# Weights in half-size pieces, and four instead of five seven-product pairs in the gate groups of a decoder layer

## The chip, the cores and the metric

The program runs on one core of a Trainium2 chip. Its engines are TensorE (PE: matmuls; PEld: its weight loads), VectorE (DVE), ScalarE (ACT), GpSimd (POOL) and SyncE (SP), which issues most of the loads. The metric is device time in microseconds (us), the median of several executions. Before the change it is 2157.74 us (three runs, 2157.62 to 2161.36).

## What is computed

One layer of a decoder on 272 positions (16 meta tokens and 256 of the sequence), model width 2048, all in float32:

```python
u = rms_norm(h, ffn1_norm_g[l])
h = h + 0.5 * swiglu(u, ffn1_w_gate[l], ffn1_w_up[l], ffn1_w_down[l])      # width 5632
u = rms_norm(h, mix_norm_g[l])
z = u @ w_in[l]
q, k, v, qi, ki, wi, xc, gate_b, gate_c, ga, gc = jnp.split(z, SPLIT_POINTS, axis=-1)
y_attn = dsa_sparse_attention(q, k, v, qi, ki, wi, k_sel) @ w_attn_branch[l]   # top 64 keys
y_conv = (gate_b * causal_depthwise_conv(gate_c * xc, conv_w[l], conv_b[l])) @ w_conv_branch[l]
merged = jax.nn.sigmoid(ga) * y_attn + jax.nn.sigmoid(gc) * y_conv
h = h + merged @ w_out[l]
u = rms_norm(h, ffn2_norm_g[l])
h = h + 0.5 * swiglu(u, ffn2_w_gate[l], ffn2_w_up[l], ffn2_w_down[l])
```

The part around the change is the gates, ga and gc, of 2048 columns each, with their branch products (y_attn and y_conv).

## The kernel before

**Precision.** Every float32 product is made of three matmuls. A weight is split into a rounded part (whi, by ACT) and the rest (wlo, by DVE); the activations are split in the same way; the three are hi x hi, hi x lo and lo x hi.

**The stream of weights.** The class `Stream` holds one list of loads (`loads`) and one of pieces to split (`subs`), in the order of use. A load brought 2048 columns (1 MB) or 1536 (768 KB) into one of RAW_BUFS = 3 buffers of 2048 columns; a piece ("unit") is at most 1024 columns, in one of four split buffers. `next()` gives the next block of weights. When it begins a unit it runs, in this order: what was put up with `early`; one due step; `split` for the unit three further on (whi on ACT, wlo on DVE); then what was put up with `later` and has come due. So the order on ACT and DVE follows from the lags of these calls, and each engine goes through its list in order. `load` issues on SP; a load waits until its buffer's last split is done.

**The stages.** FFN 1 (all 272 positions); the attention projections with the index and attention work between the units; the convolution; the gates, in four groups of 512 columns; the output projection (`po`); FFN 2. From `widen` on, in FFN 2, one more raw buffer and two more split buffers are in use.

**Pairs.** A gate group computes ga and gc for 512 columns and 256 tokens, and goes through the 2048 rows in eight pairs. A plain pair ("C") is eight products of 128x512 blocks, 24 matmuls, in two units, from one 1 MB load. A pair with seven products ("P") saves a product with sums of weights and sums of tokens: 21 matmuls, in four units, from two loads: four sums of weights (1 MB) and three plain blocks (768 KB). The sums of weights are made much earlier (`prepare`): POOL fetches a chunk, DVE does four additions of 512 columns, POOL stores it in a scratch in DRAM. Most preparations are spread over FFN 1, the last LATE of them over the projections. The sums of tokens (`sums_of_tokens`, put into the tiles made) are made by ACT and DVE in the first gate group, at given lags.

**Banks.** The eight PSUM banks of a group are q1 to q8. The seven products go to q1, q3, q5, q6, q7, q4, q2, in the order q7, q5, q6, q3, then the rest; a plain pair uses q2 and q3, then q4 and q8. After the last P pair, `recombine` copies q1 (ACT) and makes four steps on DVE, one per unit: vv from q6, vx from q7, vv from q5, ve from q5. After the eighth pair come the branch products (`pbr`), in four of the banks, 96 matmuls per group from four 1 MB loads; then `merge` on DVE: four multiplies that read these banks, two additions. The merged result of one group is transposed on TensorE inside the next (`turn_merged`, tiles pt, two blocks of four transposes in two banks); ACT and DVE then split it into ms.

Of the kernel before, what the change touches and what calls it, by code (L numbers as in the profile page):

```python
# [15 lines left out]
P = 128  # L16
# [30 lines left out]
RAW_BUFS = 3  # L47
# [13 lines left out]
SEVEN = (3, 5, 7, 1, 6)  # L61
SEVEN2 = (3, 5, 7, 1)
DOUBLES = 2
LATE = 9
# [7 lines left out]
def pairs_gate(c):  # L72
    return list(zip("CCCPPPCC", [0, 2, 4, 3, 5, 7, 6, 1]) if c == 0 else zip("PPCPPPCC", [3, 5, 0, 7, 1, 6, 2, 4]))
# [24 lines left out]
class Stream:  # L98
# [20 lines left out]
    def add(self, src, n, width):  # L119

        per = min(SUB // width, SUB // P)
        g = len(self.loads)
        self.loads.append((src, n * width))
        for k in range(0, n, per):
            self.subs.append((g, "raw", k * width, min(per, n - k), width))

    def add_pair(self, kind, four, five, ahead=None):

        if kind == "C":
            self.add(four.pop(0), 4, WIDE)  # L130
            return
        if kind == "P":
            src, made = ahead.pop(0)
            self.ahead_of.append(src)
            self.made_ahead.append(made)
            self.add(made, 4, WIDE)
            self.add(src[:, WIDE:], 3, WIDE)
            return
        g = len(self.loads)
        src = five.pop(0)  # L140
        self.loads.append((src[:, 2 * WIDE :], 3 * WIDE))
        self.added[g] = len(self.doubles)
        self.doubles.append((g, src))
        self.subs += [
            (g, "sa", 0, 2, WIDE), (g, "sb", 0, 2, WIDE),
            (g, "one", 0, 2, WIDE), (g, "last", 2 * WIDE, 1, WIDE),
        ]

    def widen(self, raw_pool, split_pool, sum_pool):

        self.raw_pools, self.raw_bufs = [raw_pool] + self.raw_pools * 3, RAW_BUFS + 1
        self.split_pools, self.ahead = [split_pool] + self.split_pools * 2, AHEAD + 2
        self.n_raw = self.n_tiles = 0
        self.sum_pool = sum_pool
        self.add_up(DOUBLES - 1)
# [38 lines left out]
    def load(self, upto):  # L194
        while self.n_loaded < min(upto, len(self.loads)):
            src, n = self.loads[self.n_loaded]
            pool = self.raw_pools[self.n_raw % len(self.raw_pools)]
            self.n_raw += 1
            raw = pool.tile([P, RAW], F32, name="raw")
            self.nc.sync.dma_start(raw[:, :n], src)  # L200
            self.raw[self.n_loaded] = raw
            self.n_loaded += 1

    def sum_ahead(self):

        add = self.nc.vector.tensor_add
        for g, kind, _, _, _ in self.subs[self.n_split : self.n_split + 2]:
            if kind == "sa" and self.sum_pool and g not in self.summed:
                self.load(g + self.raw_bufs)
                self.summed.add(g)  # L210
                raw = self.raw[g]
                sb = self.sum_pool.tile([P, 2 * WIDE], F32, name="sb", tag="sb")
                add(sb[:, :WIDE], self.sums[g, "sa"][:, WIDE:], raw[:, :WIDE])
                add(sb[:, WIDE:], sb[:, :WIDE], raw[:, 2 * WIDE : 3 * WIDE])
                self.sums[g, "sb"] = sb

    def split(self, upto):
        nc = self.nc
        while self.n_split < min(upto, len(self.subs)):
# [3 lines left out]
            g, kind, c, kk, width = self.subs[self.n_split]  # L223
            self.load(g + self.raw_bufs)
            n = kk * width
            if (g, kind) in self.sums:
                raw = self.sums.pop((g, kind))
            else:
                raw = self.raw[g][:, c : c + n]
# [63 lines left out]
def tile_decoder_layer(  # L293
# [442 lines left out]
    with ExitStack() as mix:  # L736
# [438 lines left out]
        for at, (i, to) in zip((0, 3, 7, 14, 20), made1.items()):  # L1175
            sums_of_tokens(i, gains[1], to, at)
# [15 lines left out]
        def gates(c):  # L1192
# [3 lines left out]
            def after_end(q, buf, tags):  # L1196
# [12 lines left out]
                lambda n: n == 6 and c > 0 and turn_merged(("q1", "q6")), None, after_end,  # L1209
            )  # L1210

            sides = [[[bank(tag, "pbr"), 0, KC] for tag in tags] for tags in (("q1", "q5"), ("q6", "q7"))]
# [55 lines left out]
    raw2 = ctx.enter_context(tc.tile_pool(name="raw2", bufs=1, reuse_waits="tile"))  # L1268
# [285 lines left out]
```

## Time and profile before

| | |
|---|---|
| runs | 2157.74 us, median of 3 (2157.62 to 2161.36) |
| the profiled execution | 2167.35 us; its span 2165.6 us |
| TensorE busy | 2129.0 us, 98% of the span, 12994 matmuls |
| DVE / ACT busy | 74% / 51% |
| mean granted TensorE clock | 0.995 |
| moved by DMA | 583 MB, 269 GB/s over the span |
| busy share of DVE in FFN 2 (1470 to 2150) | 568 of 680 us |

A page of the profile names engine, source line (L236 is line 236), operation and tiles as out<-in. Idle time of an engine counts only where it is the one that the end waits for. A wait is shown as "engine line <- what ended it: us in total, times, longest". In a timeline the row gives the start, the duration, and in brackets the idle time before it with what ended it.

### The profile page before, as it was taken

The page shows a single profiled execution, that of the slowest core. Times are in us where ns is not written, and L with a number is a line of the kernel's source. Part 1 is how long each engine was busy: PE and PEld are TensorE (multiplying, and loading weights), DVE is VectorE, ACT ScalarE, POOL GpSimd, SP SyncE. Part 2 cuts the span into 40 slices and gives each one's busy share as a digit, 9 for nine tenths or more (in the row PEclk, how much of TensorE's full clock was granted, in tenths as well). Part 3 has the DMA queues.
Part 4 walks back from the last instruction along what each step waited for, and adds up shares of the span by engine and source line. Part 5 has one row for each costly group of instructions (what it writes and reads, how often), then busy time and mean ns, then how long its engine had stood idle before and what let it go on. Part 6 is the DMA issues. An engine that isn't in the chain of part 4 may idle for free.

```text
span 2165.6 us, 32506 instructions
## 1 busy us (share of the span) xinstructions
PE 2129.0 (98%) x12994; PEld 1913.1 (88%) x12994; DVE 1611.4 (74%) x2108; ACT 1112.2 (51%) x1441; POOL 117.0 (5%) x182
## 2 busy tenths in 40 slices
PE   8999999999999999999999998999999999999999
PEld 8999999999999998789987776888888888888887
DVE  7777766677777757787576666587888978888887
ACT  5444433344444445465465454476666566656564
POOL 3000000000000100000000000000000000000000
PEclk9999999999999999999999999999999999999999
DMA  7788888888888867854566576467788887688774
GB/s 279 282 326 335 339 329 332 324 335 332 338 335 322 315 226 284 333 182 138 173 226 220 204 255 233 141 235 266 263 291 256 266 300 288 260 235 304 277 252 146
DMA packets 87702, 583.33 MB, mean 269 GB/s; under 512 B 9760, under 2 KB 9888, under 8 KB 27520
## 3 DMA queue, kind: packets, MB, share of 16 engines
q1 hardware_dynamic: 67680, 446.46, 57.2%
q0 software_dynamic: 19728, 134.64, 17.6%
q8 instruction: 101, 1.65, 0.3%
q14 instruction: 49, 0.40, 0.1%
q10 hardware_dynamic: 144, 0.17, 0.0%
HBM read 516.23 MB, written 65.01 MB: 268 GB/s over the span
## 4 chain that ended last, share of the span: by engine, by line
PE 89%; DVE 4%; DMA 4%; ACT 2%; issue 1%; POOL 0%; SPq 0%; ACTq 0%; DVEq 0%; POOLq 0%
PE q L627 12%; PE q L629 12%; PE q L628 12%; PE pd L418 4%; PE pd L416 4%; PE pd L417 4%; PE pu L417 4%; PE pu L418 4%; PE pu L416 4%; PE pg L417 4%; PE pg L418 4%; PE pg L416 4%; PE po L431 3%; DVE wlo L236 2%; PE po L433 1%
## 5 line engine op out<-in xcount | busy, mean ns | idle before, releaser
L236 DVE TENSOR_TENSOR wlo<-raw,whi 128x1024 fp32r<-128x1024 f32 (+1 forms) x873 | 1007.6, 1168 | 502.9 <-ACT whi L235 493.0
L235 ACT ACTIVATE whi<-raw 128x1024 fp32r<-128x1024 f32 (+1 forms) x873 | 875.0, 1013 | 927.4 <-PE q L629 248.0
L628 PE MATMUL q<-wlo,act 128*128 128x512 f32 x748 | 293.1, 392 | 2.4 <-DVE wlo L236 2.3
L627 PE MATMUL q<-whi,act 128*128 128x512 f32 x748 | 294.2, 393 | 0.8 <-ACT whi L235 0.8
L629 PE MATMUL q<-whi,act 128*128 128x512 f32 x748 | 292.7, 391 | 0.0
L416 PE MATMUL pd<-mid,whi 128*128 128x272 f32 x704 | 201.7, 286 | 0.0
L417 PE MATMUL pd<-mid,whi 128*128 128x272 f32 x704 | 201.7, 286 | 0.0
L418 PE MATMUL pd<-mid,wlo 128*128 128x272 f32 x704 | 201.7, 286 | 0.0
L416 PE MATMUL pg<-act,whi 128*128 128x272 f32 x672 | 192.7, 287 | 0.0
L417 PE MATMUL pg<-act,whi 128*128 128x272 f32 x672 | 192.5, 287 | 0.0
L418 PE MATMUL pg<-act,wlo 128*128 128x272 f32 x672 | 192.5, 287 | 0.0
L416 PE MATMUL pu<-act,whi 128*128 128x272 f32 x672 | 192.5, 286 | 0.0
L417 PE MATMUL pu<-act,whi 128*128 128x272 f32 x672 | 192.5, 286 | 0.0
L418 PE MATMUL pu<-act,wlo 128*128 128x272 f32 x672 | 192.5, 286 | 0.0
L628 PEld LDWEIGHTS q<-wlo,act 128*128 128x128 f32 x748 | 141.5, 189 | 32.6 <-DVE wlo L236 3.8
L627 PEld LDWEIGHTS q<-whi,act 128*128 128x128 f32 x748 | 141.6, 189 | 30.9 <-ACT whi L235 1.9
L180 DVE TENSOR_TENSOR prep<-prep 128x512 f32<-128x512 f32 x240 | 164.2, 684 | 5.5 <-DMA prep<-in_w2p_dram 5.5
L629 PEld LDWEIGHTS q<-whi,act 128*128 128x128 f32 x748 | 141.3, 189 | 29.7
L416 PEld LDWEIGHTS pd<-mid,whi 128*128 128x128 f32 x704 | 132.6, 188 | 0.0
L417 PEld LDWEIGHTS pd<-mid,whi 128*128 128x128 f32 x704 | 132.6, 188 | 0.0
L418 PEld LDWEIGHTS pd<-mid,wlo 128*128 128x128 f32 x704 | 132.6, 188 | 0.0
L416 PEld LDWEIGHTS pg<-act,whi 128*128 128x128 f32 x672 | 126.6, 188 | 0.0
(281 smaller groups left out, 3819.9 us busy)
## 6 DMA issues: line engine op xcount, KB each, us to landing
raw<-in_wgu_dram SPq DMA_DIRECT2D x87, 1024.0 KB, 6.7
raw<-in_w_dram SPq DMA_DIRECT2D x74, 1024.0 KB, 7.0
raw<-in_wd_dram SPq DMA_DIRECT2D x44, 1024.0 KB, 6.5
prep<-in_w2p_dram POOLq DMA_DIRECT2D x42, 1024.0 KB, 9.5
s<-prep POOLq DMA_DIRECT2D x42, 1024.0 KB, 6.7
raw<-s SPq DMA_DIRECT2D x42, 1024.0 KB, 5.8
raw<-in_w2p_dram SPq DMA_DIRECT2D x42, 768.0 KB, 5.6
raw<-in_wcv_dram SPq DMA_DIRECT2D x24, 1024.0 KB, 4.9
```

Source lines behind the costliest of these rows:

```text
L180: nc.vector.tensor_add(x[out], x[a], x[b])
L235: nc.scalar.activation(to[0], raw, AF.Copy)
L236: nc.vector.tensor_sub(to[1], raw, to[0].bitcast(F32))
L416: nc.tensor.matmul(ps, whi, xhi, start=first, stop=False)
L417: nc.tensor.matmul(ps, whi, xlo, start=False, stop=False)
L418: nc.tensor.matmul(ps, wlo, xhi, start=False, stop=last)
L431: nc.tensor.matmul(ps.rearrange("p (a t) -> p a t", a=2), whi, x(i), start=i == 0, stop=False)
L433: nc.tensor.matmul(ps[:, :SEQ], wlo, x(i)[:, 0, :], start=False, stop=i == total - 1)
L627: nc.tensor.matmul(ps, xhi, whi, start=n == 0, stop=False)
L628: nc.tensor.matmul(ps, xhi, wlo, start=False, stop=False)
L629: nc.tensor.matmul(ps, xlo, whi, start=False, stop=n == total - 1)
```

## The change

It has two parts, and their numbers.

*Loads.* Each load now brings one unit: at most 1024 columns (512 KB), or 512 columns (256 KB) where a pair's three plain blocks end. The buffers are half as large, 1024 columns, and there are six; in FFN 2 two more (eight for four). A pair with doubled weights in FFN 2 ("D") is loaded in two pieces instead of one. The bytes of a pair are the same.

*Gates.* Group 0 is as it was (CCCPPPCC). Groups 1 to 3 go from PPCPPPCC to CPPCPPCC: four P pairs instead of five, two and two, with a plain pair first. One token sum less is made (SEVEN), and the fourth at lag 16 instead of 14. 57 weight sums are prepared instead of 60, and LATE is 4 instead of 9, so 53 instead of 51 in FFN 1 and 4 instead of 9 in the projections. The transposes stand in the eighth pair, not the seventh, in banks q6 and q1; the branch products use q7 and q5, then q6 and q1.

```diff
-RAW_BUFS = 3
+RAW_BUFS = 6
...
-SEVEN = (3, 5, 7, 1, 6)
+SEVEN = (3, 5, 7, 1)
...
-LATE = 9
+LATE = 4
...
-    return list(zip("CCCPPPCC", [0, 2, 4, 3, 5, 7, 6, 1]) if c == 0 else zip("PPCPPPCC", [3, 5, 0, 7, 1, 6, 2, 4]))
+    return list(zip("CCCPPPCC", [0, 2, 4, 3, 5, 7, 6, 1]) if c == 0 else zip("CPPCPPCC", [0, 3, 5, 2, 7, 1, 4, 6]))
...
     def add(self, src, n, width):
         per = min(SUB // width, SUB // P)
-        g = len(self.loads)
-        self.loads.append((src, n * width))
         for k in range(0, n, per):
-            self.subs.append((g, "raw", k * width, min(per, n - k), width))
+            m = min(per, n - k)
+            self.subs.append((len(self.loads), "raw", m, width))
+            self.loads.append((src[:, k * width : (k + m) * width], m * width))
...
-        self.loads.append((src[:, 2 * WIDE :], 3 * WIDE))
+        self.loads += [(src[:, 2 * WIDE : 4 * WIDE], 2 * WIDE), (src[:, 4 * WIDE :], WIDE)]
...
-        self.raw_pools, self.raw_bufs = [raw_pool] + self.raw_pools * 3, RAW_BUFS + 1
+        self.raw_pools, self.raw_bufs = [raw_pool] + self.raw_pools * 3, RAW_BUFS + 2
...
-            raw = pool.tile([P, RAW], F32, name="raw")
+            raw = pool.tile([P, SUB], F32, name="raw")
...
-        for at, (i, to) in zip((0, 3, 7, 14, 20), made1.items()):
+        for at, (i, to) in zip((0, 3, 7, 16), made1.items()):
...
-                lambda n: n == 6 and c > 0 and turn_merged(("q1", "q6")), None, after_end,
+                lambda n: n == 7 and c > 0 and turn_merged(("q6", "q1")), None, after_end,
...
-            sides = [[[bank(tag, "pbr"), 0, KC] for tag in tags] for tags in (("q1", "q5"), ("q6", "q7"))]
+            sides = [[[bank(tag, "pbr"), 0, KC] for tag in tags] for tags in (("q7", "q5"), ("q6", "q1"))]
...
-    raw2 = ctx.enter_context(tc.tile_pool(name="raw2", bufs=1, reuse_waits="tile"))
+    raw2 = ctx.enter_context(tc.tile_pool(name="raw2", bufs=2, reuse_waits="tile"))
```

From `split` on, line numbers are three lower in the changed kernel (L236 is L233 there). On TensorE, at the border of gate groups 0 and 1 (pbr: branch products; made3: token sums of pair 3; act: split activations), there stood before:

```order
L629 MATMUL pbr_12282<-whi_12360,cs1_10177 128x512
L627 MATMUL pbr_12283<-whi_12360,cs1_10177 128x512
L628 MATMUL pbr_12283<-wlo_12361,cs1_10177 128x512
L629 MATMUL pbr_12283<-whi_12360,cs1_10177 128x512
L627 MATMUL q7_12428<-whi_12378,made3_11920 128x512
L628 MATMUL q7_12428<-wlo_12379,made3_11920 128x512
L629 MATMUL q7_12428<-whi_12378,made3_11920 128x512
L627 MATMUL q5_12446<-whi_12378,made3_11920 128x512
```

and now:

```order
L626 MATMUL pbr_12634<-whi_12714,cs1_10467 128x512
L624 MATMUL pbr_12635<-whi_12714,cs1_10467 128x512
L625 MATMUL pbr_12635<-wlo_12715,cs1_10467 128x512
L626 MATMUL pbr_12635<-whi_12714,cs1_10467 128x512
L624 MATMUL q2_12786<-whi_12732,act_136 128x512
L625 MATMUL q2_12786<-wlo_12733,act_136 128x512
L626 MATMUL q2_12786<-whi_12732,act_136 128x512
L624 MATMUL q3_12787<-whi_12732,act_136 128x512
```

The first matmuls of the group no longer write q7 and q5 but q2 and q3.

On DVE, in gate group 1, from the second step of the recombination (vv, vx, ve) to its last, with the split of the transposed result (ms0) and the sums at the end of the group (L1198), before:

```order
L706 TENSOR_TENSOR vv_12684<-q6_12450,va_12683 128x512
L236 TENSOR_TENSOR wlo_12719<-raw_12646,whi_12718 128x1024
L707 TENSOR_TENSOR vx_12685<-q7_12428,vv_12684 128x512
L453 TENSOR_TENSOR ms0_12707<-pt_12708,ms0_12707 128x4x128
L453 TENSOR_TENSOR ms0_12707<-pt_12713,ms0_12707 128x4x128
L236 TENSOR_TENSOR wlo_12740<-raw_12646,whi_12739 128x1024
L708 TENSOR_TENSOR vv_12684<-q5_12446,vv_12684 128x512
L1198 TENSOR_TENSOR va_12683<-q2_12476,va_12683 128x512
L1198 TENSOR_TENSOR vv_12684<-q3_12458,vv_12684 128x512
L236 TENSOR_TENSOR wlo_12761<-raw_12668,whi_12760 128x1024
L709 SCALAR_TENSOR_TENSOR ve_12686<-q5_12446,vx_12685 128x512
```

and now:

```order
L703 TENSOR_TENSOR vv_13055<-q6_12848,va_13054 128x512
L233 TENSOR_TENSOR wlo_13079<-raw_13004,whi_13078 128x1024
L704 TENSOR_TENSOR vx_13056<-q7_12834,vv_13055 128x512
L233 TENSOR_TENSOR wlo_13098<-raw_13013,whi_13097 128x1024
L705 TENSOR_TENSOR vv_13055<-q5_12844,vv_13055 128x512
L1195 TENSOR_TENSOR va_13054<-q2_12786,va_13054 128x512
L1195 TENSOR_TENSOR vv_13055<-q3_12787,vv_13055 128x512
L233 TENSOR_TENSOR wlo_13130<-raw_13025,whi_13129 128x1024
L706 SCALAR_TENSOR_TENSOR ve_13057<-q5_12844,vx_13056 128x512
L450 TENSOR_TENSOR ms0_13116<-pt_13117,ms0_13116 128x4x128
L450 TENSOR_TENSOR ms0_13116<-pt_13122,ms0_13116 128x4x128
```

The two operations on ms0 have moved from behind vx to behind ve, the last step.

On SP, at the start of the program, from the third load of weights (h: the residual stream, wgu: the first FFN's gate and up weights), before:

```order
L200 DMA raw_159<-in_wgu1_dram 128x1024
L388 DMA h_138<-in_h_dram 128x1088
L200 DMA raw_171<-in_wgu1_dram 128x2048
L388 DMA h_138<-in_h_dram 128x1088
L200 DMA raw_185<-in_wgu1_dram 128x2048
L388 DMA h_138<-in_h_dram 128x1088
L200 DMA raw_192<-in_wgu1_dram 128x2048
L200 DMA raw_247<-in_wgu1_dram 128x2048
```

and now:

```order
L197 DMA raw_156<-in_wgu1_dram 128x1024
L385 DMA h_135<-in_h_dram 128x1088
L197 DMA raw_164<-in_wgu1_dram 128x1024
L197 DMA raw_166<-in_wgu1_dram 128x1024
L197 DMA raw_168<-in_wgu1_dram 128x1024
L197 DMA raw_174<-in_wgu1_dram 128x1024
L385 DMA h_135<-in_h_dram 128x1088
L197 DMA raw_188<-in_wgu1_dram 128x1024
L385 DMA h_135<-in_h_dram 128x1088
L197 DMA raw_195<-in_wgu1_dram 128x1024
L197 DMA raw_215<-in_wgu1_dram 128x1024
```

Ahead of the next part of h there are four loads of half the size where there was one whole one. Over the whole program SP's list has 898 rows for 472.

More of the change, by code (lines that the diff above doesn't have):

```diff
@@ L140, in add_pair @@
         src = five.pop(0)
-        self.loads.append((src[:, 2 * WIDE :], 3 * WIDE))
+        self.loads += [(src[:, 2 * WIDE : 4 * WIDE], 2 * WIDE), (src[:, 4 * WIDE :], WIDE)]
         self.added[g] = len(self.doubles)
         self.doubles.append((g, src))
[L144 to L147, printed above, removed]
+        self.subs += [(g, "sa", 2, WIDE), (g, "sb", 2, WIDE), (g, "raw", 2, WIDE), (g + 1, "raw", 1, WIDE)]
     def widen(self, raw_pool, split_pool, sum_pool):
-        self.raw_pools, self.raw_bufs = [raw_pool] + self.raw_pools * 3, RAW_BUFS + 1
+        self.raw_pools, self.raw_bufs = [raw_pool] + self.raw_pools * 3, RAW_BUFS + 2
         self.split_pools, self.ahead = [split_pool] + self.split_pools * 2, AHEAD + 2
@@ L206, in sum_ahead @@
         add = self.nc.vector.tensor_add
-        for g, kind, _, _, _ in self.subs[self.n_split : self.n_split + 2]:
+        for g, kind, _, _ in self.subs[self.n_split : self.n_split + 2]:
             if kind == "sa" and self.sum_pool and g not in self.summed:
@@ L210, in sum_ahead @@
                 self.summed.add(g)
-                raw = self.raw[g]
+                one, last = self.raw[g], self.raw[g + 1]
                 sb = self.sum_pool.tile([P, 2 * WIDE], F32, name="sb", tag="sb")
-                add(sb[:, :WIDE], self.sums[g, "sa"][:, WIDE:], raw[:, :WIDE])
-                add(sb[:, WIDE:], sb[:, :WIDE], raw[:, 2 * WIDE : 3 * WIDE])
+                add(sb[:, :WIDE], self.sums[g, "sa"][:, WIDE:], one[:, :WIDE])
+                add(sb[:, WIDE:], sb[:, :WIDE], last[:, :WIDE])
                 self.sums[g, "sb"] = sb
@@ L222, in split @@
             self.sum_ahead()
-            g, kind, c, kk, width = self.subs[self.n_split]
+            g, kind, kk, width = self.subs[self.n_split]
             self.load(g + self.raw_bufs)
@@ L228, in split @@
             else:
-                raw = self.raw[g][:, c : c + n]
+                raw = self.raw[g][:, :n]
             pool = self.split_pools[self.n_tiles % len(self.split_pools)]
```

## The prediction

> **What bounds the kernel now.** I read the page first, then a table by stage, then the waits of TensorE, then the timelines of DVE, ACT and POOL at the places that these named. From the page, the span and the engines' busy time:
>
> ```profile
> span 2165.6 us, 32506 instructions
> PE 2129.0 (98%) x12994; PEld 1913.1 (88%) x12994; DVE 1611.4 (74%) x2108; ACT 1112.2 (51%) x1441; POOL 117.0 (5%) x182
> ```
>
> TensorE is busy for 98%, so only its idle time, its slow time and its instruction count matter. The windows by stage tell where it is not busy (columns: length, then busy time and count of PE, PEld, DVE, ACT, POOL, then granted clock, DMA share, GB/s):
>
> ```profile
> 0.00:40.00 40.00, 31.66 (x222) 30.50 (x223) 28.93 (x38) 24.39 (x41) 17.13 (x23) 1.00 0.87 325
> 40.00:800.00 760.00, 760.00 (x6165) 760.00 (x6164) 530.62 (x699) 313.98 (x379) 62.84 (x111) 1.00 0.84 317
> 800.00:970.00 170.00, 165.70 (x978) 143.23 (x976) 131.68 (x274) 90.90 (x167) 10.27 (x18) 0.99 0.74 268
> 970.00:1085.00 115.00, 114.97 (x829) 105.72 (x828) 76.58 (x112) 56.57 (x101) 5.93 (x6) 1.00 0.47 157
> 1085.00:1378.00 293.00, 272.86 (x1172) 219.53 (x1171) 195.54 (x219) 155.62 (x182) 0.74 (x1) 0.97 0.64 224
> 1470.00:2150.00 680.00, 680.00 (x3063) 563.86 (x3062) 568.24 (x650) 415.78 (x481) 14.06 (x16) 1.00 0.78 267
> ```
>
> The first FFN, the conv stage and the second FFN have no idle time at all. 1085 to 1378 are the gates: 20.1 us idle, and a mean clock of 0.97. 800 to 970 is the attention projections: 4.3 us idle, clock 0.99. The waits of TensorE in 1080:1380, and the largest of 800:1080:
>
> ```profile
> PE q L627 <- DVE ve L1223: 6.5, 3, 2.2
> PE pt L674 <- DVE vv L706: 6.2, 3, 2.1
> PE q L628 <- DVE wlo L236: 3.8, 5, 0.8
> PE pbr L627 <- DVE ve L709: 1.9, 1, 1.9
> PE q L627 <- ACT whi L235: 1.5, 4, 0.6
> ...
> PE pqt L904 <- DVE zz L807: 3.4, 2, 3.2
> ```
>
> The five of the gates make 19.9 us, and the change touches each of them. In the timeline of TensorE, one of the three at a group's start, and one of the short ones:
>
> ```profile
> 1161.40 0.39 PE L628 MATMUL pbr<-wlo,cs 128*128 128x512 f32 x1
> 1161.63 0.39 PE L629 MATMUL pbr<-whi,cs 128*128 128x512 f32 x1
> 1164.19 0.47 PE L627 MATMUL q<-whi,made 128*128 128x512 f32 x1 [2.18 <-DVE ve L1223]
> ...
> 1193.55 0.50 PE L627 MATMUL q<-whi,act 128*128 128x512 f32 x1
> 1194.81 0.50 PE L628 MATMUL q<-wlo,act 128*128 128x512 f32 x1 [0.76 <-DVE wlo L236]
> ```
>
> A 128x512 matmul is drawn 0.39 long, but they start 0.23 apart (1161.40, 1161.63): the step is 0.227 us. Across the wait the starts are 2.56 apart, so 2.33 us are lost where 2.18 are shown: a shown wait understates by about 0.16, the short ones by about 0.2 (1.26 less 0.23 is 1.03, shown 0.76). Beside the idle time there is slow time. Two of the windows at half clock, 3.42 us each:
>
> ```profile
> 1139.43:1142.85 3.42, 3.42 (x10) 2.64 (x9) 2.67 (x4) 2.24 (x3) 0.00 (x0) 0.50 0.13 24
> 883.43:886.85 3.42, 3.33 (x17) 3.36 (x17) 3.33 (x9) 1.03 (x1) 0.00 (x0) 0.50 0.74 268
> ```
>
> Each costs half its length, 1.7 us. A clock of 0.97 over 293 us is 8.8 us, which is five such windows in the gates; 0.99 over 170 us is one in the projections. The quoted two start right behind an idle time of 1.9 and of 3.2 us, so I take the windows to go with the waits.
>
> [...]
>
> **The change, part by part.** (a) *Start of a group.* In groups 1 to 3 the first matmul goes to bank q7, which the fourth multiply of the merge frees. The first and fourth on DVE:
>
> ```profile
> 1161.57 0.68 DVE L1223 TENSOR_TENSOR va<-pbr,va 128x512 f32<-128x512 f32 x1
> 1163.37 0.68 DVE L1223 TENSOR_TENSOR ve<-pbr,ve 128x512 f32<-128x512 f32 x1
> ```
>
> With a plain pair first, the banks are q2, q3, q4, q8, read for the last time a whole stretch of branch products earlier; q7 comes 24 matmuls later (24 x 0.227 = 5.4 us) and is now the bank of the first multiply. DVE's six merge operations (about 3.6 us at 0.6 apart) run under splits already made three units ahead (a plain unit is 12 matmuls, 2.7 us). Removed: 3 x 2.33 = 7.0.
>
> (b) *Transposes.* The second block of four waits for bank q6, freed by the recombination's vv (L706), which stands behind the split of a later unit. Twenty-four matmuls later it is long done: removed 6.2 + 3 x 0.16 = 6.7.
>
> (c) *Loads.* The waits for whi and wlo come where three seven-product pairs end. Landing times, issue by issue, and one ACT wait:
>
> ```profile
> raw<-sg SPq DMA_DIRECT2D x18, 1024.0 KB, 4.8
> raw<-in_wgp_dram SPq DMA_DIRECT2D x18, 768.0 KB, 4.2
> raw<-in_wo_dram SPq DMA_DIRECT2D x6, 256.0 KB, 2.9
> ...
> 1123.10 2.01 ACT L235 ACTIVATE whi<-raw 128x1024 fp32r<-128x1024 f32 x2 [1.78 <-DMA raw<-in_wg_dram]
> L236 DVE TENSOR_TENSOR wlo<-raw,whi 128x1024 fp32r<-128x1024 f32 (+1 forms) x873 | 1007.6, 1168 | 502.9 <-ACT whi L235 493.0
> L235 ACT ACTIVATE whi<-raw 128x1024 fp32r<-128x1024 f32 (+1 forms) x873 | 875.0, 1013 | 927.4 <-PE q L629 248.0
> ```
>
> A seven-product pair is 21 matmuls, 4.77 us, and takes two loads. With three buffers a buffer comes round every 3/2 x 4.77 = 7.15 us. It is held while the load lands (mean 4.5), for the first unit's turn on TensorE (two products, six matmuls, 1.4 us) and for the last split (1.01 + 1.17): 8.1 us. So it falls 0.9 behind per load, and three pairs in a row use up the lead. Now a pair takes four buffers of six, again one every 7.15 us, but a half lands in about 3.5 us (an estimate, on the line between 2.9 for 256 KB and 4.8 for 1 MB) and is held for one split: 5.7 us. It keeps up, and SP can issue it: four issues of 0.33 in 4.77 us.
>
> ```profile
> 1141.53 0.33 SPq L200 DMA_DIRECT2D raw<-sg  x1
> ```
>
> Also two pairs in a row instead of three bring less to keep up with. Removed 3.8 + 1.5 + 9 x 0.2 = 7.1, of which I leave 1.0 for the first group, whose order is the old one (bounds: nothing removed, all removed).
>
> (d) *Branch products of group 0.* They wait for the last recombination, behind the token sums of the fifth made pair:
>
> ```profile
> 1136.17 1.22 DVE L236 TENSOR_TENSOR wlo<-raw,whi 128x1024 fp32r<-128x1024 f32 x1
> 1137.30 0.42 DVE L652 TENSOR_TENSOR vm<-vm 128x256 f32<-128x256 f32 x1
> 1138.29 0.68 DVE L709 SCALAR_TENSOR_TENSOR ve<-q,vx 128x512 f32<-128x512 f32 x1
> ```
>
> That pair is no longer made: three small operations go, 1.0 us (1137.30 to 1138.29), of 1.9 + 0.16. Removed 1.0 (bounds 0 and 2.1).
>
> (e) *Clock.* With no wait above 1.1 us left, five windows go: 5 x 1.7 = 8.5 (bounds 3.4 and 8.5).
>
> (f) *Three pairs become plain*: 24 matmuls for 21, so 9 x 0.227 = 2.0 added. Their three preparations go too; they were hidden.
>
> (g) *The later turn.* Its two DVE operations now stand behind the last recombination, 12 matmuls before the branch products. With DVE on time, at 0.6 us for an operation of 512 and 1.2 for a split, and counted from the end of the unit before: two adds, the split, ve and the two of the turn end at 1.2, 2.4, 3.0, 3.6 and 4.2. TensorE needs the banks q5, q6 and q1 after 15, 18 and 21 matmuls, at 3.4, 4.1 and 4.8, the transposes not counted. It fits by half a microsecond, and anything late on DVE shows here. I add 1.0, near the lower end (bounds: nothing, and 3 x 2.1, as long as today's waits).
>
> (h) *Projections.* DVE waited for a preparation's load, and TensorE for DVE:
>
> ```profile
> 879.61 0.69 DVE L180 TENSOR_TENSOR prep<-prep 128x512 f32<-128x512 f32 x1 [5.48 <-DMA prep<-in_w2p_dram]
> 883.52 0.87 PE L904 MATMUL pqt<-ident,zz 128*128 128x128 f32 x3 [3.15 <-DVE zz L807]
> ```
>
> Nine preparations were spread over these units, now four: a load every two units and more. Removed 3.15 + 0.16 + 1.7 of clock = 5.0 (bounds 0 and 5.0). The first FFN takes two more, 53 for 51 in 760 us, at a DMA share of 0.84 and with TensorE never idle: cost 0. If that cover were gone, the price is the rival that is slower.
>
> (i) *Start.* SP now issues four halves instead of one whole load ahead of the second half of h: 1 MB more. At 325 GB/s that is 3.2 us; as three go out without a wait for a buffer, I take 2.5. POOL's squares follow that landing, ACT's wait for POOL, and TensorE's operands stand behind it on ACT:
>
> ```profile
> 15.25 1.63 POOL L477 TENSOR_TENSOR sq<-h 128x272 f32<-128x272 f32 x1 [0.30 <-DMA h<-in_h_dram]
> 22.79 0.43 ACT L475 ACTIVATE sq<-h 128x272 f32<-128x272 f32 x1 [3.65 <-POOL ssq L480]
> ```
>
> ACT stood 3.65 us already, so the delay passes through. Added 2.5 (bounds 0, and 3.2 with a window of 1.7).
>
> (j) *Second FFN.* Eight half buffers for four; same splits, same bytes, TensorE never idle: 0.
>
> Sum: -7.0 - 6.7 - 6.1 - 1.0 - 8.5 + 2.0 + 1.0 - 5.0 + 2.5 = -28.8. The profiled execution took 2167.35 (its span and 1.75 around it), so 2138.6 with a profile. The runs shown are 9.6 lower, at 2157.74. If all the waits are in them too, they come to 2128.9; if the 9.6 lies wholly in what goes away (c, e and h hang on landing times and on the clock's phase), to 2138.6. a and b, which hang on neither, are 13.7 of the sum, so I stay nearer to the first: 2131.
>
> **Rivals.** *The wait moves* (0.15): g costs its upper end and keeps three windows of half clock, since ve was 1.9 late in group 0 today. Against it: that lateness came behind late loads and the token sums. 2131 + 5.3 + 5.1 = 2141. *The loads stay late* (0.10): in pairs of 1.75 MB per 4.77 us TensorE asks for 385 GB/s, above any rate in the table, so that lead and not landing decides; c keeps its 7.1 and two windows: 2131 + 6.1 + 3.4 = 2141. *The clock is not tied to the waits* (0.05): e and h's window stay, 2131 + 8.5 + 1.7 = 2141. *It changes nothing that counts* (0.04): the gates' gain is given back in the second FFN, where DVE is busy 568 of 680 us: about 2157.
>
> *Halves cost their fixed part* (0.04), the slower one. By the three landing rows a load takes 2.3 us plus 2.5 per MB, so two halves take 7.1 where the whole took 4.8. If that part is not hidden, the first FFN, which eats a load in 5.8 us (760 us over 131 loads), waits 1.3 us for each: 2131 + 170 = 2301. It decides once a half takes longer than six buffers last, 17 us less the split, or if loads do not overlap. Against it: the first FFN moves 317 GB/s, more than one load at a time could.
>
> [...]
>
> **How the numbers follow.** The forecast has 0.62. Its own range is 2123 (c, d, g and i at their good ends, 5.6 off 2128.9) to 2139. The three rivals at 2141 may come with the higher of the two sums, 7.6 above mine, and the twenty additions that DVE no longer makes in the projections may free 3 us more: the range is 2120 to 2149. Above lie the no-change case and the slower one. 0.2%, about what a measurement of this kernel tells from no change, is 4.3 us: faster means below 2153.4. Faster 0.92, within 0.04, slower 0.04.
>
> **What would show it.** Right: no wait of TensorE for L1220's ve at a group's start, none of pt for vv, clock 1.00 in the gates, no half-clock window near 883, a first wait for ACT's act longer than 0.6 by some 2.5. Wrong: waits of pbr for ve or ms of about 2 us in each group, waits for whi in the gates as many as before, or any idle time between 40 and 800 or after 1470.

## The result, and the profile after

The changed kernel takes 2134.91 us (median of four runs, 2133.22 to 2136.95); four runs of the kernel before on the same chip have a median of 2159.55 (2157.62 to 2162.72). The ratio is 0.9885, with an interval of 0.9868 to 0.9902: 24.6 us or 1.15% less. The prediction was 2131 with a range of 2120 to 2149; direction and range held, the point was 3.9 us too low.

The profiled execution took 2133.22 us, with a span of 2131.4. From its page, the engines' busy time; the windows by stage (columns as in the prediction; the gates now end near 1344); and the three largest waits of TensorE:

```profile
PE 2115.5 (99%) x13003; PEld 1908.5 (90%) x13003; DVE 1599.2 (75%) x2086; ACT 1108.0 (52%) x1432; POOL 112.2 (5%) x176
```

```profile
0.00:40.00 40.00, 31.55 (x226) 30.60 (x227) 28.48 (x38) 24.54 (x41) 15.51 (x23) 1.00 0.89 329
40.00:800.00 760.00, 760.00 (x6164) 759.82 (x6162) 535.90 (x707) 314.10 (x380) 64.74 (x115) 1.00 0.89 323
800.00:970.00 170.00, 168.86 (x1019) 147.06 (x1020) 125.03 (x261) 93.94 (x172) 6.62 (x9) 1.00 0.64 212
1085.00:1350.00 265.00, 262.86 (x1178) 217.07 (x1177) 191.64 (x215) 149.76 (x172) 0.74 (x1) 1.00 0.71 236
1440.00:2115.00 675.00, 675.00 (x3041) 559.80 (x3040) 565.31 (x645) 411.51 (x475) 14.03 (x16) 1.00 0.80 267
```

```profile
PE start L413 <- ACT whi L232: 6.0, 1, 6.0
PE pbr L624 <- DVE ve L706: 2.1, 1, 2.1
PE start L415 <- DVE wlo L233: 1.1, 1, 1.1
```

Of the five waits of the gates one is left, that of the branch products in group 0. TensorE is idle for 2.1 of the 265 us from 1085 to 1350, and its clock is 1.00 in every stage: no window of half clock. From the first matmul of the gates to the first of the output projection it is 256.9 us, where it was 285.8; the first FFN ends at 793.9 (before: 794.4), and from there to the gates it is 293.0 us (298.2); the second FFN takes 692.8 in both.

The start of a group, in the timeline of TensorE; before, there were 2.56 us between the last branch product and the first matmul of the group, now 0.23:

```profile
1152.91 0.39 PE L626 MATMUL pbr<-whi,cs 128*128 128x512 f32 x1
1153.14 0.39 PE L624 MATMUL q<-whi,act 128*128 128x512 f32 x1
```

### The profile page after: what moved, and what is told of

Its sections match the earlier page's. It is cut to its first block, busy times and chain, and to the rows that moved or that the text cites. A ratio compares the mean times of both kernels' runs of the same rounds, so it can differ in the third digit from the quotient of the medians.

```text
span 2131.4 us, 33615 instructions
## 1 busy us (share of the span) xinstructions
PE 2115.5 (99%) x13003; PEld 1908.5 (90%) x13003; DVE 1599.2 (75%) x2086; ACT 1108.0 (52%) x1432; POOL 112.2 (5%) x176
## 3 DMA queue, kind: packets, MB, share of 16 engines
q0 software_dynamic: 18864, 128.35, 17.4%
## 4 chain that ended last, share of the span: by engine, by line
PE 96%; DVE 1%; DMA 1%; ACT 1%; issue 0%; POOL 0%; SPq 0%; ACTq 0%; DVEq 0%
PE q L626 13%; PE q L625 13%; PE q L624 13%; PE pd L413 4%; PE pd L415 4%; PE pd L414 4%; PE pu L414 4%; PE pg L414 4%; PE pu L415 4%; PE pg L415 4%; PE pg L413 4%; PE pu L413 4%; PE po L428 3%; PE po L430 1%; PE pbr L624 1%; PE pbr L625 1%
## 5 line engine op out<-in xcount | busy, mean ns | idle before, releaser
L233 DVE TENSOR_TENSOR wlo<-raw,whi 128x1024 fp32r<-128x1024 f32 (+1 forms) x867 | 1002.5, 1170 | 485.4 <-ACT whi L232 469.3
L624 PE MATMUL q<-whi,act 128*128 128x512 f32 x763 | 298.3, 391 | 0.0
L626 PE MATMUL q<-whi,act 128*128 128x512 f32 x763 | 297.2, 389 | 0.0
L177 DVE TENSOR_TENSOR prep<-prep 128x512 f32<-128x512 f32 x228 | 156.2, 685 | 0.0
## 6 DMA issues: line engine op xcount, KB each, us to landing
prep<-in_w2p_dram POOLq DMA_DIRECT2D x42, 1024.0 KB, 10.1
```

The costliest lines, as they stand in the source:

```text
L177: nc.vector.tensor_add(x[out], x[a], x[b])
L233: nc.vector.tensor_sub(to[1], raw, to[0].bitcast(F32))
L624: nc.tensor.matmul(ps, xhi, whi, start=n == 0, stop=False)
L626: nc.tensor.matmul(ps, xlo, whi, start=False, stop=n == total - 1)
```

## The experiments

Each ran beside runs of the kernel before on the same chip; a ratio is to those, with its interval. "Gates" is the time from the first matmul of the gates to the first of the output projection, "idle" TensorE's idle time in it, and "windows" counts those of half clock in the whole profiled execution (those in the gates in brackets). All three are of that one execution.

| kernel | median us | ratio | gates | idle | windows |
|---|---|---|---|---|---|
| before, first profile | 2159.55 | 1 | 285.8 | 20.1 | 6 (5) |
| before, second profile | | | 278.1 | 17.9 | 3 (2) |
| the change | 2134.91 | 0.9885 [0.9868, 0.9902] | 256.9 | 2.1 | 0 |
| halves alone | 2152.66 | 0.9958 [0.9944, 0.9971] | 273.6 | 14.7 | 3 (2) |
| gates alone | 2135.32 | 0.9878 [0.9860, 0.9895] | 257.3 | 1.7 | 0 |
| LATE = 9 | 2135.18 | 0.9874 [0.9860, 0.9887] | 257.6 | 2.6 | 0 |
| old turn | 2140.41 | 0.9898 [0.9885, 0.9912] | 264.6 | 7.4 | 2 (1) |
| seven-product pair first | 2136.32 | 0.9877 [0.9859, 0.9894] | 258.6 | 3.0 | 1 (0) |
| five in a row, halves | 2139.82 | 0.9893 [0.9876, 0.9909] | 262.4 | 5.0 | 2 (1) |
| five in a row, whole | 2143.57 | 0.9913 [0.9899, 0.9927] | 267.2 | 9.4 | 0 |
| sum later | 2133.13 | 0.9876 [0.9861, 0.9891] | 255.9 | 1.1 | 1 (0) |
| banks of group 0 | 2132.93 | 0.9875 [0.9858, 0.9891] | 255.8 | 1.0 | 0 |
| both of these | 2131.48 | 0.9860 [0.9833, 0.9886] | 254.8 | 0.3 | 0 |
| three halves | 2362.83 (one run) | | 318.1 | 40.5 | 20 (6) |

### The kernel before, looked at again

No edit. The question was the 9.6 us between the first profiled execution and the runs.

> The kernel before, unchanged, for a second look at where it loses time. Theory: the waits of the gates that come from the order of the instructions are the same as in the first profile (q for ve 6.5, pt for vv 6.2, pbr for ve 1.9), so they are in every execution; the wait for zz in the projections and the number of half-clock windows differ, since they hang on landing times and on the clock. A span near 2160 with two or three windows of half clock for the six of the first profile. Rival 'all the same': six windows and a wait for zz of 3.2 again, a span of 2165.

It took 2158.35 us with a profile. TensorE's largest waits, and one of the places where a window of half clock is gone:

```profile
PE q L627 <- DVE ve L1223: 6.5, 3, 2.2
PE pt L674 <- DVE vv L706: 5.3, 3, 2.2
PE q L628 <- DVE wlo L236: 3.3, 5, 0.8
PE pqt L904 <- DVE zz L807: 2.7, 2, 2.5
PE pbr L627 <- DVE ve L709: 1.6, 1, 1.6
```

```profile
1196.10:1199.51 3.41, 1.65 (x12) 1.24 (x11) 3.20 (x4) 2.63 (x4) 0.00 (x0) 1.00 0.93 317
1199.52:1202.93 3.41, 3.41 (x18) 2.83 (x17) 2.46 (x4) 0.97 (x2) 0.00 (x0) 1.00 0.87 310
```

Of the waits that come from the order, the one at a group's start is the same (6.5); that of the transposes is 0.9 shorter and that of the branch products 0.3, where all three were expected to be the same. The wait for zz is there again, 2.5 at its longest for 3.2. The whole list is 28.3 us for 32.5. The windows are three instead of six, 5.1 us less. Together that is 9.3, for 9.0 between the two profiles. So the first profile was an execution with more windows of half clock than the second, which is close to the median of the runs, and what the change saves there is three windows, not six: 2158.35 less 2133.22 is 25.1, close to the 24.6 of the runs, where the first profile gives 34.1.

### Each half of the change alone

The gates alone are the kernel before with

```diff
-LATE = 9
+LATE = 4
-    ... zip("PPCPPPCC", [3, 5, 0, 7, 1, 6, 2, 4])
+    ... zip("CPPCPPCC", [0, 3, 5, 2, 7, 1, 4, 6])
-    lambda n: n == 6 and c > 0 and turn_merged(("q1", "q6"))
+    lambda n: n == 7 and c > 0 and turn_merged(("q6", "q1"))
-    ... for tags in (("q1", "q5"), ("q6", "q7"))]
+    ... for tags in (("q7", "q5"), ("q6", "q1"))]
```

and the shorter SEVEN with its lags. The halves alone are the changed kernel with these lines undone.

> The kernel before with the half-size loads and six buffers alone; gates (PPCPPPCC, five pairs with seven products), turn, banks and LATE = 9 as before. Theory: the halves alone take the late weights away, so in the gates TensorE's waits for whi and wlo (1.5 and 3.8 us shown) are gone, while those of q for ve (6.5), of pt for vv (6.2) and of pbr for ve (1.9) stay: 7 us below before. Rival 'the order did it': the waits for whi and wlo stay at some 5 us and the time is that of before (within 2 us). Rival of the prediction 'halves cost their fixed part': idle time of TensorE in the first FFN, slower by tens of us.

> The kernel before with the change of the gates alone (CPPCPPCC, four pairs with seven products, later turn, other banks, LATE = 4); whole loads of 1 MB and 768 KB in three buffers. Theory: the waits of q for ve and of pt for vv go (7.0 and 6.7), nine matmuls come (2.0), the projections' wait for zz goes (3.3): 15 us below before; the waits for whi and wlo stay in part, 2 to 5 us shown. Rival 'the order did it': these are gone too, and it is 22 us below before, as the whole change.

TensorE's waits with the halves alone:

```profile
PE q L624 <- DVE ve L1220: 6.5, 3, 2.2
PE pt L671 <- DVE vv L703: 5.5, 3, 2.1
PE pbr L624 <- DVE ve L706: 1.7, 1, 1.7
PE q L625 <- DVE wlo L233: 0.8, 1, 0.8
PE pqt L901 <- DVE zz L804: 0.3, 1, 0.3
```

and with the gates alone:

```profile
PE pbr L627 <- DVE ve L709: 0.8, 1, 0.8
PE q L628 <- DVE wlo L236: 0.8, 1, 0.8
PE pqt L904 <- DVE zz L807: 0.3, 1, 0.3
```

Halves alone: of the 5.3 us of waits for whi and wlo 0.8 is left, with the old order of pairs; the wait for zz is gone too, with nine preparations; the three waits that come from the order stay. That is 0.42% (the ratio times 2159.55 gives 9 us; 7 expected). Gates alone: the waits for whi, wlo and zz are down to the same 0.8 and 0.3, with the whole loads in three buffers, and the time is that of the whole change: 0.9878 against 0.9885, intervals over each other. Either remedy is enough for the late weights and for the wait of the projections; together they bring no more than the gates alone. The theory that the halves take the late weights away and the rival that the order does are both right, and beside the new order the halves, most of the change's code, brought nothing that can be measured.

### What the halves are good for

The changed kernel with five pairs with seven products in a row in groups 1 to 3, with half-size and with whole loads. Both also make the fifth token sum again (at lag 22) and have LATE = 7:

```diff
-    ... zip("CPPCPPCC", [0, 3, 5, 2, 7, 1, 4, 6])
+    ... zip("CPPPPPCC", [0, 3, 5, 7, 1, 6, 2, 4])
```

> The changed kernel with five pairs with seven products in a row in groups 1 to 3 (CPPPPPCC), 60 sums, LATE = 7; half-size loads and six buffers. Theory (term c, that a half is held 5.7 us and six buffers come round every 7.15): no wait for whi or wlo even with five in a row, nine matmuls fewer, 2 us below the changed kernel. Rival 'loads stay late': five in a row ask for 385 GB/s over 24 us, which the stream does not give; waits for wlo or whi of 2 to 4 us in each group, 4 to 10 us above the changed kernel.

> The same order (CPPPPPCC, five in a row) with the whole loads of before in three buffers. Theory: a buffer is held 8.1 us and comes round every 7.15, 0.9 late per load, ten loads in a row: waits for whi and wlo of 3 to 6 us in each group, 10 to 18 us above the changed kernel and as much above the same order with halves. Rival 'the order alone did it, the halves do nothing': the same time as the same order with halves, within 2 us.

With halves, then with whole loads:

```profile
PE pbr L624 <- DVE ve L706: 2.8, 2, 2.3
PE q L625 <- DVE wlo L233: 1.8, 5, 0.8
```

```profile
PE q L628 <- DVE wlo L236: 6.4, 11, 0.8
```

With whole loads TensorE waits for wlo eleven times, with halves five times and by little. The gates take 267.2 and 262.4 us, the second with one window of 1.7, so without it the halves are worth 6.5 us in these two executions. In the medians they are worth 3.8 (2139.82 and 2143.57): the two intervals overlap a little, but each of the six runs with whole loads is slower than each of the five with halves. That is less than the 10 to 18 expected, but where five pairs stand in a row the halves count. For the version with halves the theory (no late weights, 2 us below the change) failed: it is 4.9 us above the change, as the rival had it (4 to 10), though with smaller waits than the rival's. Its gates are 5.5 longer, in spite of nine matmuls fewer (2.0 us). Besides the window these are late starts, some 30 for 11 counted from start to start, 8.8 us for 3.4; among them are 1.8 shown of late weights and 0.7 more of the wait for ve, and the rest are late by less than the profile draws as idle.

> The changed kernel with three half-size buffers for six (five for eight in the second FFN). Theory (the hold time of term c: 3.5 us for a half to land and 2.2 for its split): in the first FFN a unit is used in 2.9 us, so a buffer comes round every 8.7 and nothing is late; in the pairs with seven products a unit is used in 1.19 us, so it comes round every 3.6 for 5.7 held: 0.7 us late per unit, 2.8 per pair, up to 40 us over the gates less what the plain pairs make good. Rival 'halves cost their fixed part' in its sharp form: with so few in flight the first FFN waits too, 100 us or more in all. Rival 'the stream is far ahead': no more than 5 us anywhere.

```diff
-RAW_BUFS = 6
+RAW_BUFS = 3
```

It takes 2362.83 us. The first FFN in the windows by stage, and the landing times of its loads; then those of the changed kernel in the same stretch:

```profile
40.00:800.00 760.00, 706.51 (x5457) 690.10 (x5456) 463.32 (x630) 276.18 (x326) 52.21 (x97) 0.98 0.80 290
...
raw<-in_wgu_dram SPq DMA_DIRECT2D x164, 512.0 KB, 7.5
```

```profile
raw<-in_wgu_dram SPq DMA_DIRECT2D x158, 512.0 KB, 5.8
```

The first FFN waits (it ends 94 us later), the gates take 61 us more, the second FFN 71 (it has five buffers for eight). So the time is that of the sharp form of the rival (100 us or more in all, the first FFN waiting too). Whether a fixed part of each load is the reason is not shown: three halves also hold half the bytes of the three whole buffers of before. The arithmetic of my theory failed at the landing time: 7.5 us, not 3.5, and with the 2.2 of the splits 9.7 for a buffer that comes round every 8.7. That three halves land later than six (7.5 for 5.8) I did not expect; the preparations' 1 MB transfers run beside them in this stretch (48 of their loads, at 10.1 us from issue to landing), but what the loads wait for is not shown.

### The preparations

> The changed kernel with LATE = 9 for 4, so nine preparations in the projections and 48 in the first FFN. Theory (term h): TensorE waits some 3 us for zz in the projections again, 3 to 5 us above the changed kernel (2134.9). Rival: that wait came of one late landing and not of the number of preparations; within 1 us of the changed kernel.

```diff
-LATE = 4
+LATE = 9
```

0.9874, no slower than the change. DVE's wait for a preparation's load in the projections, which was 5.48 us before:

```profile
873.81 0.69 DVE L177 TENSOR_TENSOR prep<-prep 128x512 f32<-128x512 f32 x1 [2.19 <-DMA prep<-in_w2p_dram]
```

It is back, but at 2.19 it is covered, and TensorE waits 0.3 for zz. So with halves the number of preparations does not count, and the time is that of the rival: what TensorE waited for was the lateness of this one load. With whole loads and nine preparations the wait for zz came in both profiles of before (3.4 and 2.7 in all); with whole loads and four (the gates alone) it was 0.3, and with halves and nine (the halves alone) also 0.3. Why the load is ready earlier with halves stays open.

### The turn, and what opens a group

> The changed kernel with the transposes at their old place and in their old banks (in the seventh pair, q1 and q6) and the branch products in q1, q5, q6, q7 as before. Theory (term b): each group's second block of transposes waits for vv by some 2.1 us again, three times, 6 to 7 us above the changed kernel (2134.9); the branch products keep their wait in group 0. The start of a group stays without a wait, since it uses q2 and q3. Rival: vv now runs in time since the last two of the pairs with seven products stand alone; no wait, within 1 us.

The edit is the last two pairs of lines of the diff shown for the gates alone, undone: the place of the turn and the banks, both at once. 2140.41 us, 5 us above the two kernels of the same group of runs that lack this wait (2135.18 and 2135.32); TensorE's waits:

```profile
PE pt L671 <- DVE vv L703: 4.8, 3, 1.7
PE pbr L624 <- DVE ve L706: 2.6, 1, 2.6
```

The waits of the transposes for vv are back, 4.8 in three, and the gates take 264.6 us, or 262.9 without their window: 6.0 more than the change. Term b stands, though which of the two lines removes the wait is not shown. The window follows the wait of the branch products in group 0 (below), not one of these three.

> The changed kernel with the first two pairs of groups 1 to 3 exchanged (PCPCPPCC): a pair with seven products opens the group, all else as in the changed kernel. Theory (term a): the first matmul then writes q7, which is now the bank of the first merge multiply and not of the fourth; the branch products have just left it, so it waits for the multiply in q7 and then for q5, q6 and q3: some 1 us at each of three groups, 3 us above the changed kernel (2134.9, 0.9880 of before), less than the 7.0 of before because q7 is freed first. Rival: the bank's place among the merges does not count and the wait is 2.2 again, 7 us above. Rival 'the wait came of the late loads': no wait at all.

```diff
-    ... zip("CPPCPPCC", [0, 3, 5, 2, 7, 1, 4, 6])
+    ... zip("PCPCPPCC", [3, 0, 5, 2, 7, 1, 4, 6])
```

```profile
PE q L624 <- DVE va L1220: 1.1, 3, 0.4
```

A wait of 0.4 at each of three groups (some 1 was expected), 1.1 in all, and gates of 258.6 us, 1.7 more; the ratio (0.9877) doesn't tell it from the change. So of the 7.0 of term a more than five are not the plain pair's. Of the rest of the change, the halves don't take this wait away (6.5 with the halves alone, above); what remains and touches it is the bank: q7 is now freed by the first multiply of the merge (va in the row) instead of the fourth (ve). That is found by exclusion; no run has the new bank alone. A plain pair first takes the last 1 to 2 us. The prediction had put the whole of it on the pair and named the bank as a second reason.

### The wait that is left

In group 0 the branch products wait 2.1 us for ve. DVE ahead of it, in the changed kernel:

```profile
1122.07 0.42 DVE L649 TENSOR_TENSOR vm<-vm 128x256 f32<-128x256 f32 x1
...
1124.19 0.68 DVE L450 TENSOR_TENSOR made<-vm,made 128x512 fp32r<-128x512 f32 x1
...
1131.18 0.69 DVE L706 SCALAR_TENSOR_TENSOR ve<-q,vx 128x512 f32<-128x512 f32 x1
```

The three vm operations of the fifth sum are gone, but the fourth sum stands at a later lag than before, and so in the same stretch: its three additions (L649 to L651) and a split (L450), with DVE busy without a pause from there to ve.

When TensorE arrives has changed too. The first matmul of the gates and the first branch product, before (first profile) and now:

```profile
1092.62 0.40 PE L627 MATMUL q<-whi,act 128*128 128x512 f32 x1
1136.26 0.39 PE L627 MATMUL pbr<-whi,ys 128*128 128x512 f32 x1
```

```profile
1086.94 0.40 PE L624 MATMUL q<-whi,act 128*128 128x512 f32 x1
1129.03 0.39 PE L624 MATMUL pbr<-whi,ys 128*128 128x512 f32 x1
```

Counted from the first matmul of the gates, ve begins at 44.24 us (1131.18 in the row above) where it began at 45.67 (1138.29 in the row of the prediction), so DVE is 1.4 us earlier. But the first branch product begins at 42.09 where it began at 43.64, 1.5 earlier, since the late weights of group 0 no longer hold TensorE up. The wait stays because both moved. With the gates alone ve begins at 44.23; TensorE waits 0.8 for a late weight first, reaches the branch products at 43.35, and then waits 0.8 for ve.

> The changed kernel with the fourth sum of tokens at lag 22 for 16, so that its operations on ACT and DVE stand among the branch products of group 0 and no longer in the stretch before its last recombination. Theory: DVE's backlog there is from halves that land 5 to 6 us after their issue and from these sums together; without the sums (some 1.6 us of DVE) the wait of pbr for ve falls from 2.1 to 0.5 or less, 1.6 us below the changed kernel. Rival 'late halves alone': the wait stays at 2 us, since what precedes ve on DVE is the split of a late load.

```diff
-        for at, (i, to) in zip((0, 3, 7, 16), made1.items()):
+        for at, (i, to) in zip((0, 3, 7, 22), made1.items()):
```

> The changed kernel with the branch products of group 0 alone in q7 and q1, then q6 and q5, for q7 and q5, then q6 and q1: q5, which ve reads last, is now written from the tenth matmul on instead of the fourth. Theory: six matmuls are 1.4 us, so of the wait of 2.1 there remain 0.7, or nothing if ve is as early as in the kernel with whole loads; 1.4 to 2.1 us below the changed kernel. Rival: the wait is only moved, since all four banks are written within 2.7 us and the branch weights are late too; no difference within 0.5 us.

```diff
-    ... for tags in (("q7", "q5"), ("q6", "q1"))]
+    ... for tags in ((("q7", "q5"), ("q6", "q1")) if c else (("q7", "q1"), ("q6", "q5")))]
```

Each alone leaves a wait of 1.0 (in this order, the sum later and the banks):

```profile
PE pbr L624 <- DVE ve L706: 1.0, 1, 1.0
```

```profile
PE pbr L624 <- DVE ve L706: 1.0, 1, 1.0
```

So the fourth sum was half of the wait. Ahead of what is left with the sum gone stands a late load: in the timeline of ACT, with the sum later, the split that opens this stretch waits for it, and DVE's splits and ve follow without a pause from 1124.67 on. No run takes this load's lateness away:

```profile
1122.15 1.06 ACT L232 ACTIVATE whi<-raw 128x1024 fp32r<-128x1024 f32 x1 [1.62 <-DMA raw<-in_wg_dram]
```

> The changed kernel with both changes of group 0: the fourth sum of tokens at lag 22, and the branch products of group 0 in q7, q1, q6, q5. Each alone left a wait of pbr for ve of 1.0. Theory: the two gains add (1.1 from the sums, 1.1 from the bank), so no wait above 0.2 is left in the gates, TensorE is busy 264.9 of the 265 us from 1085 to 1350, and the time is 1 us below either alone (0.987 of before); no window of half clock behind the first 40 us, since none of its stretches of 3.4 us has 1.9 us without a matmul. Rival: another wait takes the place, of the branch products for the late halves; 263.9 of 265 as with either alone.

With both edits, the windows:

```profile
1085.00:1350.00 265.00, 264.73 (x1190) 218.91 (x1190) 192.48 (x216) 151.11 (x174) 0.74 (x1) 1.00 0.72 237
```

TensorE is busy for 264.73 of 265 us (264.9 expected; a wait of 0.3 for ms is left, the one that term g had feared). 2131.48 us, 0.9860 of before, with four runs between 2131.33 and 2131.82. It has the lowest median of all here. Its interval reaches over that of the change, but its four runs all lie below the change's lowest, and the kernel before took 2164.43 beside it, so the chip was not the faster one.

## Why the prediction was right, and where it was off

Against the two profiles of before, term by term (shown waits with the 0.16 or 0.2 for each that the prediction found them to lack):

| term | predicted | first profile | second profile |
|---|---|---|---|
| a, group start | -7.0 | -7.0 | -7.0 |
| b, transposes | -6.7 | -6.7 | -5.8 |
| c, late weights | -6.1 | -7.1 | -5.2 |
| d, branch products of group 0 | -1.0 | +0.2 | +0.5 |
| e, clock in the gates | -8.5 | -8.5 | -3.4 |
| f, nine matmuls | +2.0 | +2.0 | +2.0 |
| g, later turn | +1.0 | 0 | 0 |
| h, projections, with a window | -5.0 | -5.0 | -4.2 |
| i, start | +2.5 | +0.4 | 0 |
| sum | -28.8 | -31.7 | -23.1 |

The measured differences are 34.1 and 25.1. Of the rest 0.9 in the first is the first weights' landing (6.9, now 6.0). Much of what remains are starts too little late to be drawn as idle: from start to start the gates lose about 26 us in some 40 late starts in the first profile, and 3.4 in 11 now.

*Right.* a to a tenth and b to a tenth in the first profile and 0.9 in the second, f, and that the clock windows go with the waits: none is left in the gates. The undone turn brought b's waits back. But a's size came out right on a reason that carries the smaller part of it: the plain pair, named first, is worth the last 1 to 2 us of the 7.0, and the bank, named second, most of the rest.

*The step on the 9.6 us failed.* It left open whether the first profile's 9.6 us were an offset or lay in c, e and h, and stayed nearer to the offset. The two profiles of before differ in windows of half clock and in shorter waits, nearly all of them in what the change removes. Against it e is 5.1 short (two windows in the gates, not five), d 1.5, b, c and h 0.8 to 0.9 each; i and g give 3.5 back, and the short starts most of the rest: 25.1 for 28.8. I had held back 2.1 of the 28.8. With that 1.6 are missing; 1.7 more is the changed kernel's median over its profile (2134.91 for 2133.22), about one window, and 0.6 the second profile's distance to 2157.74. That makes the miss of 3.9.

*d failed.* The step "that pair is no longer made: three small operations go" was right as far as it went: ve begins 1.4 us earlier after the start of the gates. It took two things as fixed that moved. The prediction left the late weights of group 0 in place (1.0 of c); they went, TensorE reaches the branch products 1.5 us earlier and waits there instead, so that what c gains in group 0, d loses. And the fourth sum had been moved by two units into the stretch ahead of ve, which is worth about 1.0 (the run with the sum later).

*i was mis-sized.* The landing is later, as said, but POOL makes it up, and the sign named for it did not show: TensorE's wait for ACT's act is 0.8 where it was 0.6, not 2.5 longer. POOL in the changed kernel, where the row before was 15.25 with a duration of 1.63, and ACT's wait for it, 3.65 before:

```profile
17.02 0.66 POOL L474 TENSOR_TENSOR sq<-h 128x272 f32<-128x272 f32 x1 [2.41 <-DMA h<-in_h_dram]
...
22.66 0.43 ACT L472 ACTIVATE sq<-h 128x272 f32<-128x272 f32 x1 [3.48 <-POOL ssq L477]
```

POOL begins 1.8 later and is done at the same time, with a square of 0.66 us instead of 1.63. From the second part of h on, one of POOL's operations there takes about 1.6 us in the changed kernel (1.64), and three in each of the two profiles of before (1.62 to 1.64). That is no accident of one execution: over the first 40 us POOL is busy for 14.5 to 15.6 us in the nine profiles with half-size loads and six buffers, and for 17.1 to 17.4 in the four with whole loads. Why is not shown. What the halves cost at the start came by another way: of the nine profiles five have a window of half clock within the first 40 us (a mean granted clock of 0.96 there) and four have none (1.00); of the four with whole loads none has one (1.00). Five ninths of 1.7 us is 0.9, not 2.5.

*c was right by a wrong sum.* A half does not land in 3.5 us in the gates. Before, the 1 MB loads of sg took 4.8; now

```profile
raw<-sg SPq DMA_DIRECT2D x28, 512.0 KB, 4.6
raw<-in_wgp_dram SPq DMA_DIRECT2D x15, 256.0 KB, 3.4
```

With 4.6 and the 2.2 of the split a buffer is held 6.8 us of the 7.15 that it comes round in. That leaves 0.35, too little for five pairs in a row, as the run with them showed; two in a row don't need it, and they don't need halves either.

*h was right, with two reasons where one was given*: four preparations instead of nine end the wait with whole loads, and the halves end it with nine.

*The rivals.* "The wait moves" and "the loads stay late" did not come: no wait of pbr in groups 1 to 3, none for whi or wlo in the gates. "The clock is not tied to the waits" did not come either: the windows of the gates went with them. "Halves cost their fixed part" did not come with six buffers; with three the kernel lost 228 us, by a way that the runs do not settle.

## What to carry to other kernels

When one change holds two remedies for the same stall, price each alone: here either cured the late weights, and the one with most of the code added nothing that could be measured. A profile is one execution: before a term is priced by it, look for parts that may differ from one execution to the next (in the two profiles of before the windows of half clock, six and three, and the longest wait for zz, 3.2 and 2.5 us) and take a second profile or the spread of the runs. When work is taken off an engine's queue, read in the new order what stands in its place ahead of the waited-for instruction, and ask whether the engine that waits will arrive earlier too. When a bank is waited for, a bank that is freed earlier may do most of what a new order does.

## What the runs showed of the hardware

**The windows at half clock were 3.41 us long, and each of those in the gates of the first profile of before came behind 3.41 us in which TensorE was idle for 1.92 us or more.** In that profile six windows with a granted clock of 0.50 begin at 883.43, 1139.43, 1200.87, 1235.00, 1306.68 and 1347.64; the distances between them are 75, 18, 10, 21 and 12 times 3.413 us. Cut into stretches of this length, TensorE's idle time in one is the length less its busy time. The kernel before, the halves alone, and the changed kernel (its borders counted back from 2131.00, where, after its last matmul, the granted clock falls to 0.50):

```profile
1136.01:1139.42 3.41, 1.49 (x7) 0.91 (x6) 3.24 (x7) 2.06 (x3) 0.00 (x0) 1.00 0.63 264
1139.43:1142.85 3.42, 3.42 (x10) 2.64 (x9) 2.67 (x4) 2.24 (x3) 0.00 (x0) 0.50 0.13 24
```

```profile
1260.70:1264.11 3.41, 1.54 (x9) 1.37 (x10) 3.41 (x4) 2.14 (x3) 0.00 (x0) 1.00 0.99 360
1264.12:1267.53 3.41, 3.41 (x17) 2.83 (x16) 1.76 (x4) 1.06 (x1) 0.00 (x0) 1.00 0.87 304
```

```profile
1127.50:1130.91 3.41, 2.37 (x11) 1.64 (x9) 3.41 (x5) 1.78 (x3) 0.00 (x0) 1.00 0.79 233
1130.92:1134.33 3.41, 2.40 (x11) 1.99 (x11) 3.31 (x5) 2.00 (x3) 0.00 (x0) 1.00 0.73 246
1134.34:1137.75 3.41, 3.41 (x17) 2.83 (x16) 1.29 (x2) 2.97 (x4) 0.00 (x0) 1.00 0.60 186
```

1.92 us idle are followed by a clock of 0.50, 1.87 are not (3.41 less 1.49 and less 1.54). In the first profile of before the five windows of the gates stand behind 1.92, 1.95, 2.18, 2.18 and 1.98 us of idle time, the one of the projections behind 3.05; the stretch of the gates with the most idle time and no window behind it (from 1269.14) has 1.77. The changed kernel's wait of 2.1 us fell across a border, 1.04 and 1.01, and cost no window; with the old turn the same wait of the branch products (2.6 there) lay in one stretch, with 2.62 idle, and the next one ran at 0.51. What decides between 1.87 and 1.92 is not shown. A window is worth 1.7 us, half its length, so I estimate that a wait of 2.1 us cost 2.1 as it fell in the profile of the changed kernel, and would cost 3.8 with a window behind it. The spread of the runs goes with it: the changed kernel's four took 2133.22, 2134.17, 2135.65 and 2136.95 us at mean granted clocks of 1.000, 1.000, 0.999 and 0.998, where a window of 1.7 us lost lowers the mean by 0.0008; the version without the wait has a spread of 0.5 us.

**A half took nearly as long to land as a whole, in the first FFN and for sg in the gates.** In the first FFN 5.8 us for 512 KB (row above), where 1 MB took

```profile
raw<-in_wgu_dram SPq DMA_DIRECT2D x79, 1024.0 KB, 6.4
```

with twice as many buffers and about the same rate (323 and 317 GB/s). Halving a load freed its buffer hardly earlier there (by 0.6 us), and in the gates it was the same for sg (4.6 for 4.8). With only three half buffers a half took longer still (7.5), so here fewer buffers did not mean an earlier landing.
